# Gate and up of 18 feature tiles as seven block products, and the second gate moved to finished blocks

## The chip, the cores and the metric

The kernel runs on one core of a Trainium2 chip. Its time is the device time of one execution in microseconds; three runs of the kernel before gave 1183.9 to 1186.93 us, with a median of 1185.81 us. The engines are TensorE (PE, with its weight loads as PEld), VectorE (DVE), ScalarE (ACT), GpSimd (POOL) and SyncE (SP), which issues most transfers.

## The reference, cut to what matters

One decoder layer in float32 on 1024 tokens of width 1024: a normalization modulated by a conditioning vector, a mixer (windowed attention beside a state-space scan), a gated residual, then the part that the change touches:

```
def swiglu(h, w_gate_up, w_down):
    gu = h @ w_gate_up
    g, u = gu[..., :D_FF], gu[..., D_FF:]
    return (jax.nn.silu(g) * u) @ w_down          # D_FF = 2816 = 22 tiles of 128

h = rmsnorm(x, norm2[l]) * (1.0 + scale2) + shift2
x = x + gate2 * swiglu(h, w_gate_up[l], w_down[l])
return rmsnorm(x, final_norm)
```

`gate2` is one row of 1024 numbers, `cond @ ada_w[:, section 5]` plus a bias; it scales the columns of the down projection's result.

## The kernel before, in words

Every large matrix product is done in three partial products: an operand is split into a high part (a cast on ScalarE, line 89) and a low part (a subtraction on VectorE, line 80), and `mm3` (lines 92 to 95) multiplies high by high, high by low and low by high, each a matmul of a 128x128 weight with a 128x512 right-hand side.

The 1024 tokens are two halves of 512. The normalized and transposed input of the feed-forward part is `h2[half][kt]`: two halves, eight contraction tiles of 128, each as high and low part in the buffer FR, made by `h_tile` in `second_norm` (lines 701 to 714).

Gate and up: for a feature tile f and a half, `gate_up` (lines 721 to 733) loads and splits the gate weights and the up weights of the tile (512 KB each), runs 8 x 3 matmuls for each, and then forms SiLU of gate (ScalarE) times up (VectorE, line 83). The first four tiles (`early = 4`) do half 0 early, between other work, and half 1 in the main loop of lines 817 to 832; the other 18 tiles do both halves there. Two tiles form a pair. When a pair is done, `act_sums` makes four sums or differences of its four blocks on GpSimd, and seven blocks are stored to memory (`act_d`).

Down: the same scheme of seven products in place of eight is there already (Winograd's form of Strassen's method, on 2x2 blocks: pairs of feature tiles by token halves and by column halves of the result). `dn_weight` loads a pair's down weights, multiplies them by `gate2` on GpSimd (line 795), forms t1 to t4 on GpSimd (lines 798 to 801) and stores seven blocks (`wdn_d`). The stage after the loop runs seven products (`dna` to `dng`) of 11 steps, each step 12 matmuls on two operands read back from memory and split; at each product's end its four banks are added into the rows `yo` (lines 893 to 929), the residual `x1` is added on GpSimd, and squares for the last normalization are taken on ScalarE.

`second_gate` computes the row `gate2` in pieces behind tiles 1 to 8: loads of 512 KB of `ada_rest`, a multiply-add on VectorE (line 408), and at the end two matmuls (`gate`, lines 410 to 414).

Order: transfers issued by `dma` keep their written order on SP, and one that has to wait holds up all behind it. On the compute engines a planner at build time may take an instruction ahead of others written before it, by its estimate of when operands are ready; on the chip each engine then works in that order. Buffers are views at fixed offsets (in KB) of the large tiles FR, FP, FA, FB and GF; a tile opened on memory of a closed pool waits for all users of the old one. `Ring` hands out slots in turn.

Of the kernel before, what the change touches and what calls it, by code (L numbers as in the profile page):

```python
# [33 lines left out]
FR_N, FP_N, FA_N, FB_N, GF_N = 109 * 256 + 128, FP_MISC + 3072, 70 * 256 + 8, 6480, 92 * 256  # L34
# [3 lines left out]
def hymba_layer(ctx: ExitStack, tc: tile.TileContext, x, ada01, ada_rest, w_qk, w_vz, w_xbc,  # L38
# [483 lines left out]
    def ssd_prep(half):  # L522
# [31 lines left out]
        zh = view(FR, 108, [P])  # L554
# [4 lines left out]
        vt = view(FR, 108.5 + 0.5 * half, [P])  # L559
# [108 lines left out]
    hf_ring = ring_at(FA, 66.03125, 2, 2)  # L668
# [32 lines left out]
    def second_norm(half, xr, ss):  # L701
        xn = []
        for t in range(4):
            s1 = ring([1], "ss1", 4)
            add(s1, ss[t][:, 0:1], ss[t][:, 1:2])
            r = rstd_of(s1, D, f"r2_{half}{t}", 1)
            n = xn_buf[half][t]
            for e in range(2):
                es = slice(512 * e, 512 * e + 512)
                nc.vector.tensor_scalar(out=n[:, es], in0=xr[t][:, es], scalar1=r, scalar2=None, op0=ALU.mult)  # L710
            dma(x1_d[4 * half + t], xr[t])
            xn.append(n)
        for kt in range(KT):
            h_tile(h2[half][kt], xn, kt, g2, sh2, hf_ring([512]), f"h2{half}_{kt}", sm_bank, nc.vector.tensor_copy)
# [3 lines left out]
    wdn_d = {(j, i): DR.tile([P, 512], F32, tag=f"wdnd{j}_{i}", name=f"wdnd{j}_{i}") for j in ("b11", "b21", "b22", "t1", "t2", "t3", "t4") for i in range(NP)}  # L718
    early = 4

    def gate_up(f, half, out):
        pss = []
        for s in range(2):
            if (f, s) not in resident:
                resident[(f, s)] = load_w(w_gu[f + NF * s], [KT, P])
            h, l = resident[(f, s)]
            ps = mm_bank(f"psgu{f}{s}{half}")
            for kt in range(KT):
                t = h2[half][kt]
# [34 lines left out]
    pre = {(f, s): load_w(w_gu[f + NF * s], [KT, P]) for f, s in ((0, 0), (0, 1), (1, 0))}  # L764
    second_norm(1, xr, ss)
    flush()
    p_f1.close()
    p_g = ctx.enter_context(tc.tile_pool(name="p_g", bufs=1))
    GF = p_g.tile([P, GF_N], F32, name="GF")
    pair_ring, s_ring = ring_at(GF, 4, 8, 2), ring_at(GF, 20, 8, 2)  # L770
    bw_ring, bt_ring = ring_at(GF, 36, 8, 2), ring_at(GF, 52, 8, 2)
    gate2, grow2 = view(GF, 68, [D]), view(GF, 72, [D])
    resident = dict(pre)

    def second_gate(kks):
# [12 lines left out]


    def dn_weight(i):  # L790
        w, t = bw_ring([4, 512]), bt_ring([4, 512])
        for r in range(2):
            rows = w[:, 2 * r:2 * r + 2].rearrange("p a b -> p (a b)")
            dma(rows, w_dn[(2 * i + r) * P:(2 * i + r + 1) * P, :])
            nc.gpsimd.tensor_tensor(out=rows, in0=rows, in1=gate2, op=ALU.mult)  # L795
        b11, b12, b21, b22 = (w[:, k] for k in range(4))
        t1, t2, t3, t4 = (t[:, k] for k in range(4))
        gsub(t1, b12, b11)
        gsub(t2, b22, t1)
        gsub(t3, b22, b12)  # L800
        gsub(t4, b21, t2)
        for j, v in (("b11", b11), ("b21", b21), ("b22", b22), ("t1", t1), ("t2", t2), ("t3", t3), ("t4", t4)):
            store(wdn_d, j, i, v)

    def act_sums(i, a):
        s = s_ring([4, 512])
        a11, a12, a21, a22 = (a[:, k] for k in range(4))
        s1, s2, s3, s4 = (s[:, k] for k in range(4))
        gadd(s1, a21, a22)
        gsub(s2, s1, a11)  # L810
        gsub(s3, a11, a21)
        gsub(s4, a12, s2)
        for j, v in (("a11", a11), ("a12", a12), ("a22", a22), ("s1", s1), ("s2", s2), ("s3", s3), ("s4", s4)):
            if 2 * i >= early or j not in ("a11", "a12"):
                store(act_d, j, i, v)

    for i in range(NP):
        a = pair_ring([4, 512])
        for r in range(2):
            f = 2 * i + r  # L820
            if f < early:
                dma(a[:, r], act_d["a12" if r else "a11", i])
            else:
                gate_up(f, 0, a[:, r])
            gate_up(f, 1, a[:, 2 + r])
            flush()
            if 1 <= f <= 8:
                second_gate([f - 1])
            if 0 <= f - 10 < NP:
                dn_weight(f - 10)  # L830
# [4 lines left out]
    yo = [view(GF, 4 * t, [D]) for t in range(8)]  # L835
    x1 = [view(GF, 36 + 4 * t, [D]) for t in range(8)]
    op_ring = Ring([(FR, 48 + 4 * i) for i in range(4)] + [(FR, 4 * i) for i in range(12)] + [(FR, 64 + 4 * i) for i in range(10)])
    rawd_ring = ring_at(GF, 76, 2, 8)
    sq_ring = ring_at(GF, 68, 2, 2)
    fnb = view(GF, 72, [D])  # L840
# [7 lines left out]

    def product(ja, jb, banks, late, at):
# [4 lines left out]
        for i in range(NP):  # L854
            ab = operand(act_d[ja, i]), operand(wdn_d[jb, i])
# [10 lines left out]

    lo, hi = slice(0, 512), slice(512, 1024)
    sqs = [ring([2], "ssf", 8) for t in range(8)]

    def square(t, e):  # L870
        nc.scalar.activation(sq_ring([512]), yo[t][:, (lo, hi)[e]], AF.Square, accum_out=sqs[t][:, e:e + 1])

    def finish_row(t):
# [19 lines left out]
    p1 = product_into(mm_bank, "dna", "a11", "b11")  # L893
    flush()
    for t in range(4):
        nc.scalar.copy(yo[t][:, hi], p1[t])
    for t in range(8):
        dma(x1[t], x1_d[t])
    p2 = product_into(sm_bank, "dnb", "a12", "b21")
    for t in range(4):  # L900
        add(yo[t][:, lo], yo[t][:, hi], p2[t])
        gadd(yo[t][:, lo], yo[t][:, lo], x1[t][:, lo])
        square(t, 0)
    p6 = product_into(mm_bank, "dnc", "s2", "t2")
    dma(fnb, fnorm.partition_broadcast(P))
    for t in range(4):
        add(yo[t][:, hi], yo[t][:, hi], p6[t])
    p7 = product_into(sm_bank, "dnd", "s3", "t3")
    for t in range(4):
        add(yo[t + 4][:, hi], yo[t][:, hi], p7[t])  # L910
    p4 = product_into(mm_bank, "dne", "a22", "t4")
    for t in range(4):
        add(yo[t + 4][:, lo], yo[t + 4][:, hi], p4[t])
        gadd(yo[t + 4][:, lo], yo[t + 4][:, lo], x1[t + 4][:, lo])
        square(t + 4, 0)
    p5 = product_into(sm_bank, "dnf", "s1", "t1")
    for t in range(4):
        add(yo[t + 4][:, hi], yo[t + 4][:, hi], p5[t])
        add(yo[t][:, hi], yo[t][:, hi], p5[t])
        gadd(yo[t][:, hi], yo[t][:, hi], x1[t][:, hi])  # L920
        gadd(yo[t + 4][:, hi], yo[t + 4][:, hi], x1[t + 4][:, hi])
        square(t + 4, 1)
    p3 = product_into(mm_bank, "dng", "s4", "b22", 4, {5: lambda: [finish_row(t) for t in range(4, 8)]})
    put()
    for t in range(4):
        add(yo[t][:, hi], yo[t][:, hi], p3[t])
# [67 lines left out]
```

## Time and profile before

| | |
|---|---|
| median of three runs | 1185.81 us |
| profiled execution, its own time | 1182.94 us |
| its span | 1181.1 us |
| TensorE busy | 1145.7 us (97%), 5592 matmuls |
| VectorE, ScalarE, GpSimd busy | 604.6, 456.6, 251.5 us |
| main gate-and-up loop | about 520 to 962 us |
| down stage | 962 us to the end |

"L93" is line 93 of the kernel. A row such as `psgu<-FR` names the tile written and the tile read. Durations of matmuls overlap, so counts in a stretch of time say more than their mean. A bracket at the end of a timeline row is the idle time before the first of its instructions and what ended it.

### The profile page before, as it was taken

The numbers are of one execution on the slowest core, as the hardware profiler recorded it, in microseconds if no ns is written. First come the engines' busy times: TensorE is split into PE (matmuls) and PEld (weight loads), VectorE is DVE, ScalarE is ACT, GpSimd is POOL, SyncE is SP. The second block draws the span as 40 slices with busy tenths as digits, with TensorE's granted clock in tenths as the row PEclk, the third lists the DMA queues.
The fourth block names the chain that finished last, engine by engine and source line by source line (L and its number), as shares of the span: only waits on it lengthen the run. The fifth ranks groups of instructions, "written<-read, shape, count | busy, mean of one in ns | idle before, by whom it ended". The sixth has DMA issues, their size and how long they took to land.

```text
span 1181.1 us, 15303 instructions
## 1 busy us (share of the span) xinstructions
PE 1145.7 (97%) x5592; PEld 946.1 (80%) x5592; DVE 604.6 (51%) x1166; ACT 456.6 (39%) x883; POOL 251.5 (21%) x184
## 2 busy tenths in 40 slices
PE   7999999999999899999999999999999999999996
PEld 6789977777878687887888888888888888888885
DVE  6976278789854865473213212222212165755555
ACT  4672266665656465342111211111111145644530
POOL 0000000002100121002110117558557520200231
PEclk9999999999999999999999999999999999999998
DMA  7546544320510541336423416566566689866523
GB/s 275 183 152 223 190 152 161 111 77 18 187 37 1 193 146 55 117 125 218 157 77 119 143 57 238 211 227 237 208 237 222 221 278 351 292 208 195 168 83 143
DMA packets 80591, 197.56 MB, mean 167 GB/s; under 512 B 9170, under 2 KB 10242, under 8 KB 80388
## 3 DMA queue, kind: packets, MB, share of 16 engines
q1 hardware_dynamic: 76612, 189.40, 46.1%
q10 hardware_dynamic: 3904, 7.18, 1.8%
q8 instruction: 44, 0.72, 0.2%
q14 instruction: 31, 0.25, 0.1%
HBM read 145.68 MB, written 52.44 MB: 168 GB/s over the span
## 4 chain that ended last, share of the span: by engine, by line
PE 71%; DVE 4%; ACT 3%; POOL 1%; issue 1%; DMA 0%; SPq 0%; DVEq 0%; POOLq 0%; ACTq 0%
PE psgu L93 13%; PE psgu L95 13%; PE psgu L94 13%; PE wo L95 2%; PE wo L93 2%; PE wo L94 2%; PE psy L485 1%; DVE FB L83 1%; PE ydg L612 1%; PE dnf L95 1%; PE dnf L93 1%; PE dne L95 1%; PE dne L93 1%; PE dnd L95 1%; PE dnd L93 1%
## 5 line engine op out<-in xcount | busy, mean ns | idle before, releaser
L93 PE MATMUL psgu<-FR 128*128 128x512 f32 x704 | 275.6, 392 | 2.4 <-ACT FR L89 2.4
L95 PE MATMUL psgu<-FR 128*128 128x512 f32 x704 | 275.5, 391 | 0.0
L94 PE MATMUL psgu<-FR 128*128 128x512 f32 x704 | 275.1, 391 | 0.0
L89 ACT CAST FR<-FP 128x1024 fp32r<-128x1024 f32 (+2 forms) x75 | 76.3, 1021 | 266.0 <-DMA FP<-in_w_gu 118.2
L80 DVE TENSOR_TENSOR FR<-FP,FR 128x1024 fp32r<-128x1024 f32 (+3 forms) x83 | 100.9, 1219 | 140.3 <-ACT FR L89 139.5
L93 PEld LDWEIGHTS psgu<-FR 128*128 128x128 f32 x704 | 132.4, 188 | 30.6 <-ACT FR L89 3.3
L94 PEld LDWEIGHTS psgu<-FR 128*128 128x128 f32 x704 | 132.6, 188 | 28.3 <-DVE FR L80 0.9
L95 PEld LDWEIGHTS psgu<-FR 128*128 128x128 f32 x704 | 132.4, 188 | 28.5 <-DVE FR L80 0.8
L80 DVE TENSOR_TENSOR FR<-GF,FR 128x512 fp32r<-128x512 f32 x154 | 107.7, 737 | 80.6 <-ACT FR L89 79.8
L784 POOL TENSOR_TENSOR GF<-GF 128x512 f32<-128x512 f32 x77 | 107.8, 1415 | 90.6 <-DVE GF L83 87.5
L89 ACT CAST FR<-GF 128x512 fp32r<-128x512 f32 x154 | 89.8, 621 | 90.3 <-DMA GF<-actda 26.9
L145 POOL TENSOR_TENSOR FP<-FP 128x1 f32<-128x1 f32 (+1 forms) x40 | 28.4, 715 | 408.9 <-DVE FP L144 354.8
L83 DVE TENSOR_TENSOR GF<-GF,psgu 128x512 f32<-128x512 f32 x40 | 27.4, 685 | 150.9 <-PE psgu L95 150.9
L787 POOL TENSOR_TENSOR GF<-GF 128x512 f32<-128x512 f32 x27 | 37.0, 1389 | 289.2 <-DVE GF L83 129.8
L795 POOL TENSOR_TENSOR GF<-GF 128x1024 f32<-128x1024 f32 x22 | 60.8, 2764 | 53.3 <-DMA GF<-in_w_dn 53.3
L732 ACT ACTIVATE GF<-psgu 128x512 f32<-128x512 f32 x40 | 23.7, 593 | 118.5 <-PE psgu L95 70.5
L93 PE MATMUL psx<-FR 128*128 128x512 f32 x128 | 52.2, 408 | 0.0
L94 PE MATMUL psx<-FR 128*128 128x512 f32 x128 | 51.9, 405 | 0.0
L95 PE MATMUL psx<-FR 128*128 128x512 f32 x128 | 51.7, 404 | 0.0
L95 PE MATMUL wo<-FR 128*128 128x512 f32 x128 | 51.1, 400 | 0.0
L93 PE MATMUL wo<-FR 128*128 128x512 f32 x128 | 51.1, 402 | 0.0
L94 PE MATMUL wo<-FR 128*128 128x512 f32 x128 | 51.0, 400 | 0.0
(290 smaller groups left out, 2076.9 us busy)
## 6 DMA issues: line engine op xcount, KB each, us to landing
FP<-in_w_gu SPq DMA_DIRECT2D x52, 512.0 KB, 5.6
FP<-in_ada_rest SPq DMA_DIRECT2D x32, 512.0 KB, 4.2
actds<-GF SPq DMA_DIRECT2D x44, 256.0 KB, 2.2
GF<-in_w_dn SPq DMA_DIRECT2D x22, 512.0 KB, 4.6
wdndt<-GF SPq DMA_DIRECT2D x44, 256.0 KB, 2.3
GF<-actds SPq DMA_DIRECT2D x44, 256.0 KB, 3.9
GF<-wdndt SPq DMA_DIRECT2D x44, 256.0 KB, 3.5
GF<-actda SPq DMA_DIRECT2D x37, 256.0 KB, 3.9
```

Of the source, the lines that this page charges most:

```text
L80: nc.vector.tensor_tensor(out=out, in0=a, in1=b, op=ALU.subtract)
L83: nc.vector.tensor_tensor(out=out, in0=a, in1=b, op=ALU.mult)
L89: nc.scalar.copy(h, raw)
L93: nc.tensor.matmul(ps, lhsT=lh, rhs=rh, start=first, stop=False)
L94: nc.tensor.matmul(ps, lhsT=lh, rhs=rl, start=False, stop=False)
L95: nc.tensor.matmul(ps, lhsT=ll, rhs=rh, start=False, stop=last)
L145: nc.gpsimd.tensor_tensor(out=r, in0=r, in1=mhalf[:, 0:count], op=ALU.pow)
L485: nc.tensor.matmul(py[:, h * 64:(h + 1) * 64], lhsT=pT[:, h, b], rhs=v_sb[tk][:, 64 * g:64 * g + 64], start=(b == 0), stop=(b == nk - 1))
L732: nc.scalar.activation(out, pss[0], AF.Silu)
L784: nc.gpsimd.tensor_tensor(out=out, in0=a, in1=b, op=ALU.subtract)
L787: nc.gpsimd.tensor_tensor(out=out, in0=a, in1=b, op=ALU.add)
L795: nc.gpsimd.tensor_tensor(out=rows, in0=rows, in1=gate2, op=ALU.mult)
```

## The change

Gate and up of tiles 4 to 21 take the seven-product form too, with blocks along the contraction: the gate weights and the up weights of a tile are the two block rows, the lower and upper four contraction tiles the two block columns, and the token halves are the columns of the right-hand side. One product is 4 contraction tiles x 3 matmuls into one PSUM bank; seven of them make gate and up for both halves.

- The right-hand sides: four of the seven need sums of h2 blocks (t1 to t4). `second_norm` now also stores every block to memory (16 stores from ScalarE's queue); during the first four tiles the blocks are loaded back, and `h2_sums` makes 16 sums and splits them.
- The weights: `w_operand` makes one split operand for each product, five products ahead, four of the seven after a sum on VectorE. Raw weights are fetched ahead (`fetch`) into a ring of three.
- The outputs: `gate_up7` adds the products on VectorE (one copy and two SiLUs on ScalarE).
- `dn_weight` no longer multiplies by the gate; only t1 to t4 are stored, the plain blocks are read from the weights themselves. `act_sums` works with one set of buffers.
- Down stage: `second_gate` runs at steps of products 1 and 2, after the buffers of the gate-and-up part are given up (`open_gd`, at step 4 of product 1, behind the last stores). The products come in another order; a block that is complete except for the last product is multiplied by `gate2` and gets its residual (`residual`); the last product's right-hand blocks are multiplied by `gate2` ahead of time on GpSimd (`gated_load`), so its result is added after the gating. The rings of raw and split operands have 6 and 15 slots (before 8 and 26).

```diff
     def second_norm(half, xr, ss):
...
         for kt in range(KT):
-            h_tile(h2[half][kt], xn, kt, g2, sh2, hf_ring([512]), f"h2{half}_{kt}", sm_bank, nc.vector.tensor_copy)
+            hf = hf_ring([512])
+            h_tile(h2[half][kt], xn, kt, g2, sh2, hf, f"h2{half}_{kt}", sm_bank, nc.vector.tensor_copy)
+            nc.scalar.dma_start(h2_d[half][kt], hf)
...
+    wanted = order[3:] + [(f, s) for f in range(early, NF) for s in range(2)]
+    def fetch():
+        if wanted:
+            f, s = wanted.pop(0)
+            fetched[f, s] = raw_ring([KT, P])
+            dma(fetched[f, s], w_gu[f + NF * s])
...
     def dn_weight(i):
...
-            nc.gpsimd.tensor_tensor(out=rows, in0=rows, in1=gate2, op=ALU.mult)
...
-        for j, v in (("b11", b11), ("b21", b21), ("b22", b22), ("t1", t1), ("t2", t2), ("t3", t3), ("t4", t4)):
+        for j, v in (("t1", t1), ("t2", t2), ("t3", b12), ("t4", t4)):
             store(wdn_d, j, i, v)
...
+    def h2_sums(k):
+        b11, b12, b21, b22, t1, t2 = h2_set[k % 2]
+        for o, v, a, b in ((op_t1, t1, b12, b11), (op_t2, t2, b22, t1), (op_t3, b12, b22, b12), (op_t4, b21, b21, t2)):
+            sub(v, a, b)
+            split(o[k][:, 0], o[k][:, 1], v)
...
+    def w_operand(n):
+        f, j = divmod(n, 7)
+        f += early
+        if f >= NF:
+            return
+        g, u = fetched[f, 0], fetched[f, 1]
+        a11, a12, a21, a22 = g[:, 0:4], g[:, 4:8], u[:, 0:4], u[:, 4:8]
+        if j == 2:
+            add(s1_w, a21, a22)
+            sub(s2_w, s1_w, a11)
+        elif j == 4:
+            sub(s3_w, a11, a21)
+        elif j == 5:
+            sub(s2_w, a12, s2_w)
+        v = (a11, a12, s2_w, s1_w, s3_w, s2_w, a22)[j]
+        w = w_ring([2, 4, P])
+        split(w[:, 0], w[:, 1], v)
+        w_ops[n] = w
+        if j > 4:
+            fetch()
+    AHEAD = 5
+    rhs = (h2[0][0:4], h2[0][4:8], op_t2, op_t1, op_t3, h2[1][4:8], op_t4)
+    def gate_up7(f, out0, out1):
+        u = u_ring([512])
+        for j in range(7):
+            n = 7 * (f - early) + j
+            w_operand(n + AHEAD)
+            w, ps = w_ops.pop(n), (mm_bank, sm_bank)[n % 2](f"psg7_{j}_{f}")
+            for k in range(4):
+                mm3(ps, w[:, 0, k], w[:, 1, k], rhs[j][k][:, 0], rhs[j][k][:, 1], k == 0, k == 3)
+            if j == 0:
+                nc.scalar.copy(u, ps)
+            elif j == 1:
+                add(c11, u, ps)
+                nc.scalar.activation(c11, c11, AF.Silu)
+            elif j == 2:
+                add(u, u, ps)
+            elif j == 3:
+                add(u4, u, ps)
+            elif j == 4:
+                add(out1, u4, ps)
+                add(u, u, ps)
+            elif j == 5:
+                add(u4, u4, ps)
+                nc.scalar.activation(u4, u4, AF.Silu)
+                mul(out1, out1, u4)
+            else:
+                add(out0, u, ps)
+                mul(out0, out0, c11)
...
             if f < early:
                 dma(a[:, r], act_d["a12" if r else "a11", i])
+                h2_sums(f)
+                if f + 2 < 4:
+                    h2_load(f + 2)
+                gate_up(f, 1, a[:, 2 + r], lambda s: early_then(f, s))
             else:
-                gate_up(f, 0, a[:, r])
-            gate_up(f, 1, a[:, 2 + r])
+                gate_up7(f, a[:, r], a[:, 2 + r])
             flush()
-            if 1 <= f <= 8:
-                second_gate([f - 1])
-            if 0 <= f - 10 < NP:
-                dn_weight(f - 10)
+            if 0 <= f - 9 < NP:
+                dn_weight(f - 9)
...
+    def open_gd():
+        flush()
+        p_g.close()
+        return ctx.enter_context(tc.tile_pool(name="p_gd", bufs=1)).tile([P, GD_N], F32, name="GD")
...
+    def residual(t, e, eng=None):
+        es = (lo, hi)[e]
+        (eng or gmul)(rows[t][e], rows[t][e], gate2[:, es])
+        gadd(rows[t][e], rows[t][e], x1[t][:, es])
...
+    p1 = product_into(mm_bank, "dna", "a11", "b11", 0, {4 + 2 * kk: lambda kk=kk: second_gate(kk) for kk in range(4)})
...
+    p2 = product_into(sm_bank, "dnb", "a12", "b21", 0, {2 * kk - 7: lambda kk=kk: second_gate(kk) for kk in range(4, 8)})
...
+    p5 = product_into(sm_bank, "dnd", "s1", "t1", 0, {i: lambda i=i: gated_step(i) for i in range(NP)})
...
+    p7 = product_into(sm_bank, "dne", "s3", "t3", 0, late_steps)
     for t in range(4):
+        add(yc[t], ya[t], p7[t])
+        add(ya[t], yd[t], p7[t])
+        residual(t + 4, 1)
+        residual(t, 1)
+        square(t + 4, 1)
...
+    p3 = product_into(mm_bank, "dng", "s4", "b22g", 4, {5: lambda: [finish_row(t) for t in range(4, 8)]})
```

## Rows read from the trace of the kernel before

**Rows 1.** The page: busy time, and 40 slices (tenths; GB/s).
```profile
PE 1145.7 (97%) x5592; PEld 946.1 (80%) x5592; DVE 604.6 (51%) x1166; ACT 456.6 (39%) x883; POOL 251.5 (21%) x184
...
PEclk9999999999999999999999999999999999999998
...
GB/s 275 183 152 223 190 152 161 111 77 18 187 37 1 193 146 55 117 125 218 157 77 119 143 57 238 211 227 237 208 237 222 221 278 351 292 208 195 168 83 143
```

**Rows 2.** The page: the chain that ended last, by engine and by line.
```profile
PE 71%; DVE 4%; ACT 3%; POOL 1%; issue 1%; DMA 0%; SPq 0%; DVEq 0%; POOLq 0%; ACTq 0%
PE psgu L93 13%; PE psgu L95 13%; PE psgu L94 13%; PE wo L95 2%; PE wo L93 2%; PE wo L94 2%; PE psy L485 1%; DVE FB L83 1%; PE ydg L612 1%; PE dnf L95 1%; PE dnf L93 1%; PE dne L95 1%; PE dne L93 1%; PE dnd L95 1%; PE dnd L93 1%
```

**Rows 3.** Windows: length, each engine's busy us (instructions), clock, DMA share, GB/s.
```profile
800.00:900.00 100.00, 100.00 (x443) 82.77 (x442) 21.89 (x20) 15.16 (x19) 65.22 (x38) 1.00 0.60 219
...
1000.00:1100.00 100.00, 100.00 (x443) 82.81 (x442) 62.95 (x97) 51.60 (x92) 6.49 (x4) 1.00 0.72 236
```

**Rows 4.** Tile psgu: ns min/median/max, first and last start.
```profile
L95 PE MATMUL psgu<-FR x704: 388/389/792, 404.3 to 962.3; 128*128 128x512 f32 x176
```

**Rows 5.** Timeline of PE from 555: start us, us, instruction, [idle before].
```profile
556.30 0.79 PE L93 MATMUL psgu<-FR 128*128 128x512 f32 x1 [2.08 <-ACT FR L89]
556.88 0.63 PE L94 MATMUL psgu<-FR 128*128 128x512 f32 x1
...
559.00 0.63 PE L95 MATMUL psgu<-FR 128*128 128x512 f32 x1
559.43 0.55 PE L93 MATMUL psgu<-FR 128*128 128x512 f32 x1
559.81 0.39 PE L94 MATMUL psgu<-FR 128*128 128x512 f32 x1
```

**Rows 6.** Lines L80, L83, L784 (700 to 940), L80 (990 to 1140), page's cast.
```profile
L80 DVE TENSOR_TENSOR FR<-FP,FR x22: 1224/1226/3454, 714.7 to 936.4; 128x1024 fp32r<-128x1024 f32 x22
...
L83 DVE TENSOR_TENSOR GF<-GF,psgu x22: 675/687/689, 701.7 to 930.2; 128x512 f32<-128x512 f32 x22
...
L784 POOL TENSOR_TENSOR GF<-GF x61: 1279/1291/2287, 703.8 to 940.0; 128x512 f32<-128x512 f32 x61
...
L80 DVE TENSOR_TENSOR FR<-GF,FR x125: 679/691/1779, 990.0 to 1137.9; 128x512 fp32r<-128x512 f32 x125
...
L89 ACT CAST FR<-GF 128x512 fp32r<-128x512 f32 x154 | 89.8, 621 | 90.3 <-DMA GF<-actda 26.9
```

**Rows 7.** Timeline of DVE from 527.
```profile
527.27 0.69 DVE L80 TENSOR_TENSOR FR<-FA,FR 128x512 fp32r<-128x512 f32 x1
532.78 0.69 DVE L83 TENSOR_TENSOR GF<-GF,psgu 128x512 f32<-128x512 f32 x1 [4.82 <-PE psgu L95]
...
543.38 0.69 DVE L83 TENSOR_TENSOR GF<-GF,psgu 128x512 f32<-128x512 f32 x1 [1.08 <-PE psgu L95]
```

**Rows 8.** Timeline of SP's queue from 528.
```profile
528.10 0.80 SPq L71 DMA_DIRECT2D GF<-actda  x2
```

**Rows 9.** The page: transfers, count, KB each, median us to landing.
```profile
FP<-in_w_gu SPq DMA_DIRECT2D x52, 512.0 KB, 5.6
...
actds<-GF SPq DMA_DIRECT2D x44, 256.0 KB, 2.2
...
GF<-actds SPq DMA_DIRECT2D x44, 256.0 KB, 3.9
```

**Rows 10.** Line L615, a transfer issued from ScalarE.
```profile
L615 ACTq DMA_DIRECT2D FA<-gzd x8: 326/326/327, 148.1 to 435.4; - x8
```

**Rows 11.** Line L408, the second gate's multiply-add.
```profile
L408 DVE SCALAR_TENSOR_TENSOR GF<-FP,GF x7: 1281/1285/1287, 552.9 to 665.5; 128x1024 f32<-128x1024 f32 x7
```

**Rows 12.** Timeline of DVE from 955.
```profile
958.65 4.76 DVE L80 TENSOR_TENSOR FR<-GF,FR 128x512 fp32r<-128x512 f32 x7 [4.91 <-ACT FR L89]
963.33 0.68 DVE L83 TENSOR_TENSOR GF<-GF,psgu 128x512 f32<-128x512 f32 x1
```

**Rows 13.** Tile dng, the last product.
```profile
L95 PE MATMUL dng<-FR x44: 388/389/389, 1142.5 to 1171.8; 128*128 128x512 f32 x44
```

More of the change, by code (lines that the diff above doesn't have):

```diff
@@ L667, in hymba_layer @@
     wot_ring = Ring([(FA, 52), (FB, 22)])
-    hf_ring = ring_at(FA, 66.03125, 2, 2)
+    h2_d = [[DR.tile([P, 512], F32, tag=f"h2d{half}_{kt}", name=f"h2d{half}_{kt}") for kt in range(KT)] for half in range(2)]
     sq_half = view(FB, 12, [512])
@@ L731, in gate_up @@
             pss.append(ps)
+            if then:
+                then(s)
         nc.scalar.activation(out, pss[0], AF.Silu)
@@ L764, in hymba_layer @@
     pre = {(f, s): load_w(w_gu[f + NF * s], [KT, P]) for f, s in ((0, 0), (0, 1), (1, 0))}
+    order = [(f, s) for f in range(early) for s in range(2)]
+    wanted = order[3:] + [(f, s) for f in range(early, NF) for s in range(2)]
+    fetched = {}
+    def fetch():
[3 more added lines that the diff above has]
+            dma(fetched[f, s], w_gu[f + NF * s])
+    for _ in range(3):
+        fetch()
     second_norm(1, xr, ss)
@@ new lines, in h2_sums, with early_load @@
+    def h2_sums(k):
[3 more added lines that the diff above has]
+            split(o[k][:, 0], o[k][:, 1], v)
+    resident = dict(pre)
+    def early_load(n):
+        if n < len(order):
+            hl = ws_ring([2, D])
+            h, l = (hl[:, j].rearrange("p (a b) -> p a b", a=KT) for j in range(2))
+            split(h, l, fetched.pop(order[n]))
+            resident[order[n]] = h, l
+            fetch()
@@ L817, in hymba_layer, with early_then @@
+    def early_then(f, s):
+        nonlocal w_ring
+        early_load(2 * f + 3 + s)
+        if f == early - 1:
+            if s == 0:
+                k0 = ws_ring.i
+                w_ring = Ring([(FR, ws_ring.slots[(k0 + d) % 3][1] + e) for d in range(3) for e in (0, 4)] + [(FR, 16 + 4 * k) for k in range(4)])
+            for n in ((0, 1, 2, 3), (4,))[s]:
+                w_operand(n)
+    w_ring = None
+    h2_load(0)
+    h2_load(1)
     for i in range(NP):
@@ L891, in product_into, with gates @@
         return p
-    p1 = product_into(mm_bank, "dna", "a11", "b11")
-    flush()
-    for t in range(4):
-        nc.scalar.copy(yo[t][:, hi], p1[t])
-    for t in range(8):
+    def gates():
+        gate(5, [gate2[:, 0:512], gate2[:, 512:1024]], grow2)
+    p1 = product_into(mm_bank, "dna", "a11", "b11", 0, {4 + 2 * kk: lambda kk=kk: second_gate(kk) for kk in range(4)})
+    ya, yb, yc, yd = ([view(GD, 8 * t + 2 * k, [512]) for t in range(4)] for k in range(4))
+    rows = [(yb[t], yd[t]) for t in range(4)] + [(yc[t], ya[t]) for t in range(4)]
```

153 lines of the change are left out of this document (94 added, 59 removed).

## The prediction, made before the changed kernel ran

> **What bounds the kernel now.** I read the page's busy shares first, then the slices, the chain of waits, then a table by windows, because a busy share does not say at what rate an engine works. TensorE is busy 97% of the span and granted full clock in nearly every slice [rows 1]; the chain runs through it for 71%, and three lines of gate-and-up matmuls (`psgu`) are 13% each [rows 2]. The reader must not take a matmul's duration, 389 ns [rows 4], as its price: matmuls overlap. The window 800 to 900 holds 443 of them in 100 us with TensorE never idle [rows 3], so one costs 100/443 = 0.2257 us. The down stage keeps the same pace (443 in 1000 to 1100, [rows 3]). In both stages VectorE is far from full: 22 and 63 of 100 us. So what counts is the number of matmuls, as long as VectorE, ScalarE and the transfers keep their operands ahead of them.
>
> **What goes.** A feature tile before is 2 halves x 2 (gate, up) x 8 contraction tiles x 3 partial products = 96 matmuls; after, 7 products x 4 x 3 = 84. For tiles 4 to 21 that is 18 x 12 = 216 matmuls fewer, 216 x 0.2257 = 48.8 us, all on the chain. A new tile takes 84 x 0.2257 = 19.0 us of TensorE (before 21.7), one product 2.71 us.
>
> A second gain: at 556.30 TensorE had stood 2.08 us for a weight cast, and its next seven steps took 559.81 - 556.30 = 3.5 us instead of 7 x 0.226 = 1.6 [rows 5]: a gap of 2.1 us cost 4.0. There the in-order transfer queue issues loads of the second gate's rows ahead of the next weights. After, these rows are loaded in the down stage and weights are fetched ahead, so I take 4.0 off; if something new is late there, nothing.
>
> **What comes on VectorE in a new tile.** Operands: seven low parts and four sums, SBUF to SBUF, 11 x 0.69 the 128x512 split of [rows 6]; outputs: seven additions from PSUM and two multiplications, 9 x 0.69 the L83 row of [rows 6]. 20 x 0.69 = 13.8 us of 19.0. Before it was two splits of 1.23 and two multiplications, 3.8 us. ScalarE gets seven casts, a copy and two SiLUs, ten operations of some 0.62 us the cast in [rows 6], far below 19. Operands are made five products (13.6 us) ahead and eight PSUM banks take turns, so single waits are covered; the cover is gone only if VectorE's average passes 19.0 us.
>
> It can be pushed there by GpSimd. A 128x1024 split takes 1.226 us at the median but up to 3.454 us in the window where GpSimd is busiest, while operations that read PSUM stay within 675 to 689 ns [rows 6]. So 13 of the 20 new operations can be held up by a GpSimd subtraction (1.29 us, [rows 6]), seven cannot. In tiles 9 to 19 GpSimd has per pair of tiles 2 x 4 subtractions of down weights and 4 of activations, 12 x 1.29 = 15.5 of 38 us, 41%. A random meeting costs half a subtraction: 13 x 0.41 x 0.65 = 3.4 us, VectorE 17.2 of 19.0. At worst all six subtractions of a tile stand in its way: 13.8 + 7.7 = 21.5 us, 2.5 us too much in 11 tiles, 27 us. At best nothing. Between 0 and 27 I take 1, since the likely 17.2 is below 19.0.
>
> The Trainium skill (SBUF — State Buffer, Who interferes with whom) says why: VectorE and GpSimd share one port pair, an exclusive lock that a VectorE instruction with two SBUF inputs contends for with a GpSimd instruction that reads SBUF, and the loser blocks fully. The rows above agree, with 3.454 us for a split that takes 1.226 alone. By this rule the change replaces long, sparse operations by many that need the lock, and it is the strongest thing against it; what it would cost is the rival B below.
>
> **The first four tiles.** They keep 192 matmuls (43 us), but VectorE now makes the right-hand operands beside them: 4 x (4 sums + 4 low parts) = 32 x 0.69 = 22 us, with five weight splits of 1.23, four multiplications and the first seven operand steps: 22 + 6.2 + 2.8 + 4.8 = 35.8 us. The normalized blocks go out through memory and come back: the last is done at 527.27 + 0.69 = 528.0, and at 528.1 the queue could first write the new buffers [rows 7, 8]; a store (2.2) and a load (3.9, [rows 9]) put the first sums at 534. The tiles end near 565 (532.8 + 3 x 10.8 by the multiplications, [rows 7], without the gap). Two splits fit before 534, so 33 us stand against 31: VectorE ends 2 us late. But the first new product needs the plain blocks alone, and the last of the sums are due 16 us later. What could be late are weights behind the sums in the queue. Bounds 0 and 4 us (a gap like that of [rows 5]); I take 1. The 16 stores issue from ScalarE at 0.33 us [rows 10], where each waits beside 1.06 us of VectorE per block: nothing.
>
> **The down stage** keeps its 924 matmuls. The second gate's eight steps of 1.29 us [rows 11] lie beside products 1 and 2, in which 22 splits take 15 of 29.8 us. Its 4 MB replace the x1 loads there, which had the queue at 351 GB/s in a slice [rows 1]; a product wants 5.8 MB in 29.8 us, 193 GB/s, plus 0.5 MB every two steps (5.4 us), 97: 290 GB/s, below that.
>
> One new wait counts. At the fifth step of product 1 the queue stores the last activation sums, then loads into buffers that overlie the old ones, and every operand from the sixth step on is behind it. After the last matmul (962.3 + 0.4, [rows 4]) come an addition, a multiplication, a subtraction (0.7 + 0.7 + 1.3), the store 2.2, two issues, the load 3.9, a cast and a low part: about 13 us. TensorE has five steps, 13.5 us. Bounds 0 and 4 us; I take 1. For the order I go by the trace: seven splits of the next stage stand ahead of the last multiplication on VectorE [rows 12], so independent work is moved forward past such waits.
>
> Applying the gate to blocks puts 12 multiplications on GpSimd and 4 on VectorE (0.7 us each) at product ends, and 11 on GpSimd for the last operand. After product 5 of the written order (`dne`) that is 16 GpSimd operations, 20.6 us; if each of some 16 splits waits for one (0.69 + 1.29), VectorE is 7 splits short in 32 us, and the ring of 15 operands covers 7. Cost 0, without that cover 5. After the last matmul (1171.8, [rows 13]) the same additions, squares, scalings and stores follow: 9.3 us of the span as before.
>
> **The sum.** Against the profiled execution (1182.94 us: span 1181.1 and 1.84 around it): 1182.94 - 48.8 - 4.0 + 1 + 1 + 1 = 1133.1. It was 2.9 us below the median of the runs, 1185.81, so I predict 1136.
>
> **Rivals.** B, the lock decides: VectorE needs 21.5 us in tiles 9 to 19, TensorE waits for operands there, +27 at the bound: 1162, half of it 1149. For it the 3.454 us row and 41% GpSimd; against it the median of 1.226 us with GpSimd busier than it will be (about 65% in the window 800 to 900, [rows 3]). Chance 0.13.
> C, two or three gaps of the kind in [rows 5] (first tiles, the queue's wait in product 1, the first product), 4 us each with the slower clock behind it: 1136 - 3 + 3 x 4 = 1145, or 1141 with two. For it the margins of -2 and +0.5 us; against it the five-product lead. Chance 0.13.
> D, slower: VectorE passes 21.7 us per tile, TensorE's old time, so that it stops in every product and does not come back to full clock. At the lower level, 1.2 of 2.4 GHz, a step took about 0.43 us [rows 5], a tile 84 x 0.43 = 36 us; in half of each of 11 tiles that is 11 x 8.6 = 94 us: 1230. It decides only if all GpSimd operations and more hit, and a slower TensorE gives VectorE time to catch up. Chance 0.04.
> E, better: nothing of the three unit terms comes, and the other transfers shift favourably: 1129 to 1132 or less. Chance 0.04. That the number of matmuls does not fall is excluded by the code.
>
> **How the numbers follow.** The forecast, 1131 to 1141, has 0.65; B and C 0.13 each, D and E 0.04, and 0.01 lies between B and D. The range reaches from E to the half of B: 1129 to 1152. A measurement tells 0.3%, 3.6 us, from no change: faster 0.95 (forecast, B, C, E), same 0.01, slower 0.04 (D).
>
> **What would show it.** 216 matmuls fewer at an unchanged pace of 443 per 100 us between the last of the first four tiles and product 1; VectorE busy 73 to 90% there; no gap at the place of [rows 5]; longest splits of 2 us beside GpSimd without TensorE waiting; the five steps of product 1 just covering the store. It is wrong if TensorE waits for VectorE's low parts in tiles 9 to 19, or the granted clock falls inside the stage.

## The result and the profile after

The changed kernel took 1147.72 us (median; runs 1144.76, 1144.90, 1150.54, 1150.87), the kernel before, timed beside it, 1185.49 us. The ratio is 0.968, 95% interval 0.9645 to 0.9719. 37.8 us are gone; the forecast was 49.8. The time lies in the range (1129 to 1152) but above the forecast's own (1131 to 1141). Its profiled execution took 1144.76 us, with a span of 1143.0.

The page of the changed kernel, engines and the granted clock by slice; before: [rows 1].

```profile
PE 1105.0 (97%) x5376; PEld 912.4 (80%) x5376; DVE 842.6 (74%) x1490; ACT 517.2 (45%) x1007; POOL 244.6 (21%) x185
...
PEclk9999999999999969999999999999999999999998
```

There are 216 matmuls fewer, as counted, and VectorE is 74% busy where it was 51%. One slice, the 15th (400 to 429 us), shows a clock of 6 where every slice before had 9; it is the first sign of what went wrong.

Windows of the changed kernel: length, busy us of PE, PEld, DVE, ACT and POOL (instructions), granted clock, DMA share, GB/s; before: [rows 3].

```profile
640.00:880.00 240.00, 240.00 (x1060) 198.75 (x1059) 203.51 (x253) 75.41 (x125) 107.74 (x68) 1.00 0.57 197
800.00:900.00 100.00, 100.00 (x443) 82.79 (x442) 82.85 (x102) 30.31 (x51) 44.00 (x28) 1.00 0.56 192
1000.00:1100.00 100.00, 98.83 (x435) 81.29 (x434) 76.30 (x97) 50.52 (x90) 40.72 (x27) 1.00 0.73 240
```

In the stage of 18 tiles TensorE never stops, at the old pace of 443 in 100 us. In the down stage it lost 1.2 us in one window.

What the matmuls waited for, 395 us to the end, changed kernel (us in total, times, longest), gate-and-up and down products:

```profile
PE psgu L94 <- DVE FR L179: 1.3, 3, 0.5
PE psgu L94 <- ACT FR L90: 1.1, 1, 1.1
PE dna L94 <- ACT FR L90: 1.1, 1, 1.1
PE dnf L94 <- ACT FR L90: 0.9, 1, 0.9
PE psgu L96 <- DVE FR L81: 0.5, 1, 0.5
PE dnf L95 <- DVE FR L81: 0.2, 1, 0.2
```

No wait of the new products (`psg`) is among them. Cut at the start of the first gate-and-up matmul, then at the start of the last matmul of each stage, the two spans divide like this:

| stretch | before, us | after, us | difference |
|---|---|---|---|
| start to first gate-and-up matmul | 402.6 | 412.2 | +9.6 |
| to the end of the first four tiles | 166.3 | 164.3 | -2.0 |
| 18 tiles | 393.4 | 342.7 | -50.7 |
| down stage | 209.4 | 214.3 | +4.9 |
| tail | 9.3 | 9.4 | +0.1 |

The middle came as forecast; 14.5 us were lost at its two ends. The loss at the first shows on ScalarE. Timeline (start, us, instruction, [idle before]) of the kernel before, ScalarE, then TensorE; the rows `ps_h` make the normalized blocks, and the first of them is the first block:

```profile
398.72 1.45 ACT L190 ACTIVATE FA<-ps_h,FP 128x512 f32<-128x512 f32 x2 [4.68 <-PE ps_h L184]
...
401.48 1.03 ACT L89 CAST FR<-FP 128x1024 fp32r<-128x1024 f32 x1
402.42 1.45 ACT L190 ACTIVATE FA<-ps_h,FP 128x512 f32<-128x512 f32 x2
403.75 1.05 ACT L89 CAST FR<-FP 128x1024 fp32r<-128x1024 f32 x1
...
402.57 0.50 PE L93 MATMUL psgu<-FR 128*128 128x512 f32 x1 [0.28 <-ACT FR L89]
```

The same of the changed kernel:

```profile
400.45 1.45 ACT L191 ACTIVATE FA<-ps_h,FP 128x512 f32<-128x512 f32 x2 [4.68 <-PE ps_h L185]
401.26 1.00 ACTq L718 DMA_DIRECT2D h2d<-FA  x2
402.31 1.45 ACT L191 ACTIVATE FA<-ps_h,FP 128x512 f32<-128x512 f32 x2 [0.40 <-PE ps_h L185]
...
411.08 2.96 ACT L90 CAST FR<-FP 128x1024 fp32r<-128x1024 f32 x3
...
412.21 0.79 PE L94 MATMUL psgu<-FR 128*128 128x512 f32 x1 [1.14 <-ACT FR L90]
```

Before, the first weight casts stood between the blocks of `second_norm`; now all eight blocks with their stores, and six instructions of the scan, come first, and the casts at 411.08 follow without a wait of their own. TensorE runs short of work meanwhile. Windows 410 to 420, of the kernel before:

```profile
410.00:415.00 5.00, 5.00 (x30) 4.06 (x29) 4.94 (x7) 1.20 (x3) 1.61 (x2) 1.00 0.91 306
415.00:420.00 5.00, 5.00 (x25) 4.18 (x25) 3.73 (x6) 3.35 (x5) 0.63 (x1) 1.00 0.58 220
```

and of the changed one, where TensorE stood still for a third of the time and the clock is at its lower level, 0.50 of full (1.2 of 2.4 GHz), before it comes back (it was at 0.50 in 400 to 405 us already, where the kernel before had 1.00):

```profile
410.00:415.00 5.00, 3.27 (x10) 1.82 (x8) 3.96 (x6) 4.05 (x6) 1.30 (x2) 0.50 0.00 0
415.00:420.00 5.00, 5.00 (x19) 4.54 (x19) 1.85 (x3) 0.00 (x0) 1.61 (x1) 0.50 0.31 105
420.00:425.00 5.00, 5.00 (x18) 3.93 (x18) 3.85 (x6) 1.02 (x4) 0.70 (x1) 0.73 0.40 118
```

### The profile page after: what moved, and what is told of

It reads as the page before. It is cut to its first block, busy times and chain, and to the rows that moved or that the text cites. A ratio compares the mean times of both kernels' runs of the same rounds, so it can differ in the third digit from the quotient of the medians.

```text
span 1143.0 us, 15497 instructions
## 1 busy us (share of the span) xinstructions
PE 1105.0 (97%) x5376; PEld 912.4 (80%) x5376; DVE 842.6 (74%) x1490; ACT 517.2 (45%) x1007; POOL 244.6 (21%) x185
## 5 line engine op out<-in xcount | busy, mean ns | idle before, releaser
L81 DVE TENSOR_TENSOR FR<-FP,FR 128x512 fp32r<-128x512 f32 (+4 forms) x244 | 195.0, 822 | 68.8 <-ACT FR L90 68.3
L90 ACT CAST FR<-FP 128x512 fp32r<-128x512 f32 (+3 forms) x236 | 157.7, 682 | 185.6 <-PE psg L95 79.8
L94 PE MATMUL psg<-FR 128*128 128x512 f32 x306 | 119.0, 389 | 0.0
L95 PE MATMUL psg<-FR 128*128 128x512 f32 x306 | 119.0, 389 | 0.0
L96 PE MATMUL psg<-FR 128*128 128x512 f32 x306 | 119.0, 389 | 0.0
L87 DVE TENSOR_TENSOR GF<-GF,psg 128x512 f32<-128x512 f32 x126 | 84.2, 680 | 30.4 <-PE psg L96 27.9
L90 ACT CAST FR<-GF 128x512 fp32r<-128x512 f32 x77 | 47.4, 619 | 79.8 <-PE psg L95 54.5
L94 PE MATMUL psg<-GR,FR 128*128 128x512 f32 x198 | 77.0, 389 | 0.0
L95 PE MATMUL psg<-GR,FR 128*128 128x512 f32 x198 | 77.0, 389 | 0.0
L96 PE MATMUL psg<-GR,FR 128*128 128x512 f32 x198 | 77.0, 389 | 0.0
L95 PEld LDWEIGHTS psg<-FR 128*128 128x128 f32 x306 | 57.4, 188 | 12.0
L94 PEld LDWEIGHTS psg<-FR 128*128 128x128 f32 x306 | 57.4, 188 | 11.9
L96 PEld LDWEIGHTS psg<-FR 128*128 128x128 f32 x306 | 57.4, 188 | 11.9
L803 POOL TENSOR_TENSOR GD<-GD 128x512 f32<-128x512 f32 x23 | 35.7, 1562 | 119.7 <-ACT GD L415 57.7
L94 PE MATMUL psgu<-FR 128*128 128x512 f32 x128 | 51.6, 407 | 2.5 <-DVE FR L179 1.3
L94 PE MATMUL psx<-FR 128*128 128x512 f32 x128 | 52.2, 408 | 0.0
L96 PE MATMUL psgu<-FR 128*128 128x512 f32 x128 | 51.4, 403 | 0.5 <-DVE FR L81 0.5
L95 PE MATMUL psx<-FR 128*128 128x512 f32 x128 | 51.8, 405 | 0.0
```

What stands on the lines that cost most here:

```text
L81: nc.vector.tensor_tensor(out=out, in0=a, in1=b, op=ALU.subtract)
L87: nc.vector.tensor_tensor(out=out, in0=a, in1=b, op=ALU.add)
L90: nc.scalar.copy(h, raw)
L94: nc.tensor.matmul(ps, lhsT=lh, rhs=rh, start=first, stop=False)
L95: nc.tensor.matmul(ps, lhsT=lh, rhs=rl, start=False, stop=False)
L96: nc.tensor.matmul(ps, lhsT=ll, rhs=rh, start=False, stop=last)
```

## The experiments

All ratios are to the kernel before, timed beside each kernel on the same chip. Not all of them ran on one chip, so two kernels are compared by their ratios, and they differ where the intervals don't overlap. Only one execution of each kernel has a profile.

**The changed kernel once more**, as the base of what follows.

> The changed kernel unchanged, for comparison on one chip. Its four runs lie at 1144.8, 1144.9 and 1150.5, 1150.9. Theory (the slower clock after the late weight casts of the first gate-and-up tile lasts longer or shorter from run to run): two groups again, some 6 us apart, median 1145 to 1151. Rival (scatter from elsewhere): one group.

1146.01 us (1144.98 to 1147.66), ratio 0.9673 [0.9657, 0.9688]. The two groups of times of the first measurement did not return. The shape is the same: gate and up from 411.6, the new tiles from 577.0, `dna` without a gap, `dnf` 33.3 us.

**The ring of four alone.** `second_norm` of the change also gave the blocks four buffers for two, which the prediction had not seen.

```diff
-    hf_ring = ring_at(FA, 66.03125, 2, 2)
...
+        hf_ring = Ring([(FA, 66.03125), (FA, 68.03125)] + ([(FA, 10), (FA, 12)], [(FA, 32), (FA, 34)])[half])
```

> The kernel before with nothing but the ring of four blocks in second_norm (two before), no stores to memory. Theory A: the ring lets ScalarE make the normalized blocks one after another, and the planner puts the first weight casts behind all eight; TensorE starts the first gate-and-up matmul near 410 us in place of 402.6, at the lower clock level: 5 to 9 us slower than before, 1191 to 1195. Theory B (the stores on ScalarE's queue and their traffic are what costs): within 1.5 us of before, 1184 to 1187.

1188.26 us, ratio 1.0029 [1.0016, 1.0043]: 2.7 us slower than the kernel before. The first gate-and-up matmul started at 407.92:

```profile
398.66 4.80 ACT L190 ACTIVATE FA<-ps_h,FP 128x512 f32<-128x512 f32 x7 [4.68 <-PE ps_h L184]
...
406.81 1.06 ACT L89 CAST FR<-FP 128x1024 fp32r<-128x1024 f32 x1
...
407.92 0.50 PE L93 MATMUL psgu<-FR 128*128 128x512 f32 x1 [1.81 <-ACT FR L89]
```

With two buffers casts stood between the blocks; with four, seven blocks run together and the casts come behind. That the planner had filled ScalarE's stops between blocks with casts is inferred from this order. So the ring alone moves the casts, 5.3 us later, and half of that reaches the end. The order is that of theory A, at about half its price; the time lies between the two that were expected.

**The ring and the stores**, both put into the kernel before.

```diff
+            nc.scalar.dma_start(h2_d[half][kt], hf)
```

> The kernel before with the ring of four blocks and the 16 stores of blocks to memory from ScalarE's queue (nothing reads them). The ring alone cost 2.7 us (e1). Theory (ring and stores together make the loss ahead of the first tiles): the first gate-and-up matmul starts at 411 to 412 us as in the changed kernel (402.6 before, 407.9 with the ring alone), and the time is 1192 to 1196. Rival (the stores add nothing; the rest of the loss comes from the other edits): 1187 to 1190.

1190.81 us, ratio 1.0042 [1.0028, 1.0055], 5.0 us slower than the kernel before; the first matmul started at 412.74, as late as in the changed kernel (412.21). ScalarE, then TensorE:

```profile
401.00 1.45 ACT L190 ACTIVATE FA<-ps_h,FP 128x512 f32<-128x512 f32 x2 [4.68 <-PE ps_h L184]
...
412.74 0.80 PE L93 MATMUL psgu<-FR 128*128 128x512 f32 x1 [0.68 <-ACT FR L89]
```

This confirms the place; the price lies between the two that were expected, and the interval overlaps that of the ring alone, so a price of the stores by themselves is not shown in the time.

**The first weights ahead of the blocks**, in the changed kernel.

```diff
     xr, ss = out_proj(0)
+    resident.update({(0, s): load_w(w_gu[NF * s], [KT, P]) for s in range(2)})
     second_norm(0, xr, ss)
```

> The changed kernel with the gate and up weights of tile 0 loaded and split before second_norm of half 0; ring and stores stay. Theory A: the casts stand ahead of the blocks, TensorE starts on the first blocks and keeps its clock: 6 to 10 us faster than the changed kernel, 1136 to 1141, in one group of times. Theory B: the stores stay, so the loss stays: within 2 us of the changed kernel.

1140.30 us, ratio 0.9615 [0.9599, 0.9631]: 5.7 us faster than the changed kernel, with intervals apart and just under the 6 to 10 expected. The first matmul is back at 403.24, behind the first two blocks, and the first four tiles end at 571.5 (576.5). ScalarE, then TensorE:

```profile
401.64 1.45 ACT L191 ACTIVATE FA<-ps_h,FP 128x512 f32<-128x512 f32 x2 [4.82 <-PE ps_h L185]
...
403.24 0.78 PE L94 MATMUL psgu<-FR 128*128 128x512 f32 x1
```

This kernel, called the early-weights kernel below, is the base of the later ones.

**No sums on GpSimd.** In the changed kernel `act_sums` and the sums of `dn_weight` are left out, and other blocks are stored in their places.

> The changed kernel without the GpSimd sums of act_sums and dn_weight in the main loop; the raw blocks are stored in their place (same transfers), so these sums are left out of the result. Theory of the prediction: the long splits beside GpSimd are covered by the five-product lead; the splits fall to 0.69 us each, VectorE's busy share between 640 and 880 us falls from 86% to about 75%, and the time stays within 2 us of the changed kernel (a microsecond may go at the step 5 wait of product 1, where one subtraction is in the chain). Rival (the lock paces the stage): 5 us or more faster.

1144.78 us, ratio 0.9663 [0.9646, 0.9680]; against 1146.01 for the changed kernel that is 1.2 us, and the intervals overlap. The window without GpSimd's sums:

```profile
640.00:880.00 240.00, 240.00 (x1061) 198.79 (x1060) 160.94 (x253) 76.42 (x125) 0.00 (x0) 1.00 0.58 196
```

The splits of line 81 in it, in ns (min/median/max):

```profile
L81 DVE TENSOR_TENSOR FR<-GF,FR x49: 684/686/694, 641.6 to 870.1; 128x512 fp32r<-128x512 f32 x49
...
L81 DVE TENSOR_TENSOR GF<-FP,GF x12: 682/683/687, 653.7 to 863.2; 128x512 f32<-128x512 f32 x12
```

The same lines of the changed kernel, and GpSimd's sums in it:

```profile
L81 DVE TENSOR_TENSOR FR<-GF,FR x50: 676/684/1782, 640.2 to 875.5; 128x512 fp32r<-128x512 f32 x50
...
L81 DVE TENSOR_TENSOR GF<-FP,GF x12: 677/1778/1786, 656.1 to 866.8; 128x512 f32<-128x512 f32 x12
...
L797 POOL TENSOR_TENSOR GF<-GF x62: 1286/1736/1834, 653.9 to 871.4; 128x512 f32<-128x512 f32 x62
```

The long splits, up to 1.78 us, are gone and VectorE is busy 160.9 us in place of 203.5 (67%, where about 75% was expected), but TensorE does the same number of matmuls. Rival B falls: VectorE and GpSimd do hold each other up (GpSimd's sums have a median of 1.74 us, before 1.29 [rows 6]), and here it costs nothing that can be measured.

**The second gate later**, in the early-weights kernel, so that the loads which wait for the stores don't stand ahead of the sixth step's.

```diff
-    p1 = product_into(mm_bank, "dna", "a11", "b11", 0, {4 + 2 * kk: lambda kk=kk: second_gate(kk) for kk in range(4)})
+    p1 = product_into(mm_bank, "dna", "a11", "b11", 0, {6 + 2 * kk: lambda kk=kk: second_gate(kk) for kk in range(3)})
...
+    p2 = product_into(sm_bank, "dnb", "a12", "b21", 0, {2 * kk - 6: lambda kk=kk: second_gate(kk) for kk in range(3, 8)})
```

> e2 (early weights) with the second gate's rows loaded two steps later: from step 6 of product 1, the last at step 8 of product 2. Theory (the queue's wait for the last activation store keeps the sixth step's operands 1.1 us too long): product 1 runs without a gap, 29.9 us in place of 31.2, and the time falls by about 1.3 us, to 1139. Rival (the transfers are the limit there, not the wait): the gap only moves, same time as e2 (1140.3) within 0.5 us.

1138.30 us, ratio 0.9605 [0.9591, 0.9619], 2.0 below the early-weights kernel (1.2 by the ratios) with overlapping intervals. It does not decide: in the early-weights kernel's own profile `dna` has no gap either, so there was nothing to remove.

**The squares later**, in the early-weights kernel. In the changed kernel ScalarE stands in `dnf` (the sixth product) before each of four squares; line 1014, ScalarE:

```profile
1078.38 0.63 ACT L1014 ACTIVATE GD<-GD 128x512 f32<-128x512 f32 x1 [3.99 <-POOL GD L800]
...
1085.17 0.63 ACT L1014 ACTIVATE GD<-GD 128x512 f32<-128x512 f32 x1 [5.04 <-POOL GD L800]
...
1090.61 0.63 ACT L1014 ACTIVATE GD<-GD 128x512 f32<-128x512 f32 x1 [4.71 <-POOL GD L800]
...
1096.50 0.63 ACT L1014 ACTIVATE GD<-GD 128x512 f32<-128x512 f32 x1 [4.13 <-POOL GD L800]
...
1097.13 2.16 ACT L90 CAST FR<-FP 128x512 fp32r<-128x512 f32 x4
```

Behind the last, VectorE and TensorE wait for these casts:

```profile
1091.88 3.44 DVE L81 TENSOR_TENSOR FR<-FP,FR 128x512 fp32r<-128x512 f32 x2 [6.18 <-ACT FR L90]
```

```profile
1097.79 0.51 PE L94 MATMUL dnf<-FR 128*128 128x512 f32 x1 [0.95 <-ACT FR L90]
1098.51 0.50 PE L95 MATMUL dnf<-FR 128*128 128x512 f32 x1 [0.22 <-DVE FR L81]
```

The edit wrote the squares at the ninth step of the product:

```diff
-        square(t + 4, 1)
-    p4 = product_into(sm_bank, "dnf", "a22", "t4")
+    p4 = product_into(sm_bank, "dnf", "a22", "t4", 0, {9: lambda: [square(t + 4, 1) for t in range(4)]})
```

> e2 with the squares of the four rows that wait for GpSimd taken at step 9 of the next product in place of its start. Theory (ScalarE is held by these squares, each waiting for four GpSimd operations, and the casts stand behind them): product dnf runs in 29.9 us in place of 31.7, time down by about 1.7 us, to 1138.6. Rival (VectorE short of splits because of the lock, as the prediction had it): the gap stays, since the GpSimd operations stay; within 0.5 us of e2.

1139.20 us, ratio 0.9614 [0.9600, 0.9629]. The planner put the squares back ahead of the casts (1072.25 to 1090.39), and a gap of 1.31 us in `dnf` remained. The edit did not take effect and tells nothing.

**The residuals in another order**, in the early-weights kernel: first the four rows that are squared, then the other four, so that each square waits for two GpSimd operations in place of four.

```diff
         residual(t + 4, 1)
-        residual(t, 1)
         square(t + 4, 1)
+    for t in range(4):
+        residual(t, 1)
```

> e2 with the residuals at the end of product dne in another order: first the four rows whose squares ScalarE takes, then the other four; same operations. In e5 the planner put the squares ahead of the casts again, so it did not tell. Theory (ScalarE held by squares that wait for GpSimd): the last square comes some 12 us after the product in place of 23, and product dnf takes 30 to 30.5 us in place of 34.9 (e2): time 1136 to 1138. Rival (VectorE short of splits because GpSimd holds the port, the same number of operations): dnf stays at 32 us or more, 1139 to 1141.

1138.56 us, ratio 0.9601 [0.9586, 0.9617], which overlaps that of the early-weights kernel. TensorE's wait for ScalarE in `dnf`, 0.4 to 1.3 us in all nine profiles with the old order, is gone; its wait for VectorE is 1.6 us. `dnf` takes 32.1 us against 34.9 in the early-weights kernel and 29.9 for a plain product, but that alone shows no gain: the nine profiles with the old order lie between 31.1 and 34.9. VectorE, ahead of its late splits:

```profile
1085.90 9.84 DVE L81 TENSOR_TENSOR FR<-FP,FR 128x512 fp32r<-128x512 f32 x9 [6.19 <-ACT FR L90]
```

It stood 6.19 us for a cast that comes behind the last square (1084.63, some 20 us after the product, where 12 were expected); then the first four of the nine splits took 1.74 to 1.77 us each, the others 0.68. So both theories have a part: the squares still hold the casts, and the splits behind them are long beside GpSimd as well. How the rest divides stays open.

**Eight buffers for the second half's blocks**, in the early-weights kernel, since in the changed kernel's `second_norm(1)` ScalarE waits 1.1 to 2.1 us for stores to land before it may write a buffer again.

```diff
-([(FA, 10), (FA, 12)], [(FA, 32), (FA, 34)])[half])
+([(FA, 10), (FA, 12)], [(FA, 32), (FA, 34), (FB, 0), (FB, 2), (FB, 6), (FB, 8)])[half])
```

> e2 with eight buffers for the normalized blocks of half 1 (four before), so that none waits for its store. Theory (ScalarE waits up to 2 us for the landing of stores while the queues are full): the block stage of half 1 takes 9 to 10 us in place of 13.5, and the first tiles end 1.5 to 3 us earlier: 1137.5 to 1139. Rival (the planner, given more buffers, puts weight casts behind the blocks as it did in half 0): same or slower than e2, up to 1144.

1141.34 us, ratio 0.9626 [0.9610, 0.9641]: no gain. The blocks of half 1 did come faster: ScalarE makes them in 10.6 us where it took 12.4 (9 to 10 expected), and TensorE's waits for them (line 179) fell from 1.1 to 0.2 us. But its waits for VectorE's low parts (line 81) rose from 1.7 to 2.3, and the first four tiles end at 571.9 against 571.5. So the stores are not what bounds the end of the first tiles.

**Half of the sums.** In the early-weights kernel t3 and t4 of the right-hand sides are not computed, and t1 and t2 are multiplied in their places.

```diff
-        for o, v, a, b in ((op_t1, t1, b12, b11), (op_t2, t2, b22, t1), (op_t3, b12, b22, b12), (op_t4, b21, b21, t2)):
+        for o, v, a, b in ((op_t1, t1, b12, b11), (op_t2, t2, b22, t1)):
```

> e2 with only t1 and t2 of the h2 sums made; t3 and t4 (16 VectorE operations of 0.69 us, 11 us, and 8 casts) are left out, t1 and t2 stand in for them, so these two products are left out of the result. Theory (VectorE, busy 94% between 550 and 575 us, makes the low parts of the last early weights late): the waits for L81 in the first tiles, 1.7 us with the slower clock behind them, go, and the first tiles end 2 to 4 us earlier: 1136.5 to 1138.5. Rival (the weights' transfers behind the h2 loads are late): the waits stay, within 1 us of 1140.3.

Windows of the early-weights kernel, then of this one (columns as above):

```profile
550.00:575.00 25.00, 23.30 (x102) 18.61 (x101) 23.40 (x33) 13.17 (x22) 6.76 (x4) 1.00 0.73 258
```

```profile
550.00:575.00 25.00, 25.00 (x112) 20.71 (x111) 21.11 (x27) 10.73 (x18) 8.22 (x5) 1.00 0.71 254
```

VectorE was 94% busy there and TensorE lost 1.7 us; with half the sums VectorE is 84% busy, TensorE loses nothing, and the first tiles end at 568.5 (571.5). The profile shows that VectorE is the bound of the first tiles' end. The time does not follow: 1140.86 us (1137.94 to 1143.85), ratio 0.9617 [0.9597, 0.9637], against 1140.30. The profiled execution here was the fastest of its four, that of the early-weights kernel the slowest of its five (1141.71), and the runs of either scatter by 4 to 6 us; whether the 3 us reach the end stays open.

**Three edits together**: early weights, the later second gate, the squares and the eight buffers.

> e2 with all three of e4, e5 and e6. If the three gaps are independent the gains add: 1.3 + 1.7 + 2, 1135 to 1136, faster than both kernels and at the forecast of 1136. If one of them only hides another, 1138 or more.

1138.25 us (1135.57 to 1141.52), ratio 0.9606 [0.9586, 0.9625]: no better than the later second gate alone, as the other two had gained nothing in time.

**The best of them**: early weights, residuals in the new order, the second gate from the sixth step on.

```diff
+    p1 = product_into(mm_bank, "dna", "a11", "b11", 0, {6 + 2 * kk: lambda kk=kk: second_gate(kk) for kk in range(3)})
...
+    p2 = product_into(sm_bank, "dnb", "a12", "b21", 0, {max(0, 2 * kk - 7): lambda kk=kk: second_gate(kk) for kk in range(3, 8)})
```

> e2 with the residual order of e9 and the second gate's rows from step 6 of product 1 (the last at step 7 of product 2). If the gains of early weights, residual order and the freed step add: 1135 to 1137.5, faster than the kernel before and the changed kernel. If run-to-run shifts of the clock ahead of the first tiles cover it: 1138 to 1140.

1137.09 us (1136.58 to 1138.67), ratio 0.9588 [0.9574, 0.9602]. It beats the kernel before by 48.7 us and the changed kernel's second timing by 8.9. Against the early-weights kernel the intervals still overlap, so a gain of the two further edits is not shown. Its waits in the down stage are down to one:

```profile
PE dnf L95 <- DVE FR L81: 0.4, 1, 0.4
```

## Why the prediction was right, and where its sizes were off

**What goes: right.** By the starts of matmuls one costs 0.2267 us, in place of the 0.2257 taken from a count per window, which includes those that overlap its edges. 216 x 0.2267 = 49.0 us; with the second gate's matmuls, which moved out of the stage (1.3 us), that is 50.3 of the 50.7 measured.

**What comes on VectorE: right.** 203.5 of 240 us is 85%, inside the 73 to 90% given. Per tile of 19.0 us that is 16.1 us, without GpSimd 160.9 / 240 x 19.0 = 12.7 (the sum had 17.2 and 13.8); so meetings with GpSimd take 3.4 us a tile, the number of the sum. The Trainium skill (SBUF — State Buffer, Who interferes with whom) has the loser of the lock on the ports that the two share block fully; splits of 1.78 us that shrink to 0.69 without GpSimd agree. Their price to the end, forecast as 1, was nothing that could be measured: TensorE has no wait in the stage, and the 1.2 us of the two medians lie within overlapping intervals. That the five products of lead are what covers it was not tested; no run changed them.

**The first four tiles: near in sum by luck (-2.0, forecast -4 + 1).** The gap of [rows 5] is gone, and VectorE is late at their end, as the 33 against 31 us said. But the stretch in the table is short because it starts late: with the ring and the stores alone, in the kernel before, it is 164.1 us too, and in the early-weights kernel 168.3. It is fairer to count from the first block, since what comes ahead of the blocks shifts by itself. In us, from the profiles:

| kernel | first block at | to the first gate-and-up matmul | to the last matmul of the four tiles |
|---|---|---|---|
| before | 398.7 | 3.8 | 170.2 |
| ring of four alone | 398.7 | 9.3 | 173.8 |
| ring and stores | 401.0 | 11.7 | 175.8 |
| changed | 400.5 | 11.8 | 176.1 |
| early weights | 401.6 | 1.6 | 169.9 |
| early weights, half of the sums | 401.1 | 1.6 | 167.5 |

So the changed kernel loses 5.9 us here, and the ring and the stores alone lose 5.6. With the start repaired 0.3 us are gained, and without half of the sums 2.7 of the 3 forecast: VectorE's lateness, priced at 1, costs 2.4 for that half. The step that failed is the sentence on the 16 stores, "where each waits beside 1.06 us of VectorE per block: nothing". It costed the stores by their 0.33 us of issue and not by what they and the two added buffers do to the order on ScalarE: the casts of the first weights went behind all eight blocks, 7.9 us more between the first block and the first matmul, and TensorE at half clock for much of the time to about 425. In time, the ring and the stores together cost 5.0 us in the kernel before, and early weights gave back 5.7: this is about half of the 12 us between forecast and result.

The other 1.7 of the 9.6 us at the first matmul are there before the blocks. The first block stands at 398.7 in both profiles without the stores and between 399.6 and 405.0 in the twelve with them. In each of the twelve the granted clock is below 1.00 somewhere ahead of 390 us (changed kernel: 0.91 in 40 to 60 us, before 1.00), ahead of anything that the ring or the stores edit, and in the other two it is not. The cause was not tested, and a shift of some 5 us that differs from profile to profile also blurs every comparison of single executions.

**The down stage: +4.9, of which 1.3 is the moved matmuls; forecast +1.** The wait in product 1 came as described, but the 13 us were 14.7. Queue of transfers, then TensorE, changed kernel:

```profile
922.06 3.07 SPq L72 DMA_DIRECT2D actds<-GF  x4
927.27 0.34 SPq L72 DMA_DIRECT2D GD<-in_ada_rest  x1
927.66 0.53 SPq L72 DMA_DIRECT2D FP<-actda  x1
```

```profile
934.29 1.19 PE L94 MATMUL dna<-FR 128*128 128x512 f32 x4 [1.06 <-ACT FR L90]
```

From the end of gate and up (919.6) to the sixth step at 934.29 are 14.7 us, against 13.5 of cover: 1.06 us and a slow start, in some executions only (the second profile of the changed kernel has none). In `dnf` the step that failed is "Cost 0, without that cover 5": the ring of 15 operands was counted against VectorE's splits, but what stood first was ScalarE, whose casts came behind squares that waited for GpSimd; VectorE waited for these casts. It cost 1.8 us in this profile and 3.4 in the second.

**The sum.** On the profiled execution the forecast change was -49.8 (1182.94 to 1133.1), the measured one -38.2 (to 1144.76). The difference of 11.6 is +1.7 ahead of the blocks, +8.9 from there to the end of the first four tiles (+5.9 for -3), -1.9 in the stage (1.3 of moved matmuls and 0.6 of pace and rounding), -1 for the lock, +3.9 in the down stage (4.9 - 1) and +0.1 in the tail; that makes 11.7, with rounding. That the time lies in the range is in part luck: the range was wide because of B and C, B did not come, and half of the miss arose ahead of the first tiles, by an order on ScalarE that no rival named. Rival C's number (1141 to 1145) was nearer than the forecast, but only one of its gaps came in this form, that in product 1. D is excluded by the stage without a wait, and E by the two ends. The four runs of the first timing lie in two pairs, 1144.8 and 1150.7, and the slower pair has the lower mean clock (0.980 and 0.983 against 0.987 and 0.990); in the second, four lie between 1145.0 and 1147.7, and their clocks do not order them. What parts them was not found.

## What to carry to other kernels

Where a planner orders the engines, read for each edited line which instructions filled its stalls: giving a stage more buffers can take away the stalls, and what stood in them, here the casts that the next stage starts with, goes behind it. Price an added operation at the engine's queue, by what is in line behind it, and not by its own duration. VectorE at 85%, slowed by GpSimd, cost nothing here where its consumer was five products behind, but TensorE lost 1.7 us in 25 where VectorE was at 94%. When single executions are compared, count from an instruction that both kernels have just ahead of the edit, here the first block, and not from the start of the span.

## What the runs showed of the hardware that was not expected

- Meetings of VectorE and GpSimd are not random: of the 12 subtractions `GF<-FP,GF` in 640 to 880 us 10 took 1.77 to 1.79 us, while the splits `FR<-GF,FR` beside them kept a median of 684 ns. The operation recurs at one place of the loop and meets GpSimd there most times; the sum had taken half a subtraction per random meeting, and came out right as a mean.
- TensorE's start can come 5.3 us later with only 2.7 us at the end (the ring alone). In the profiles 1.8 us are given back before the first four tiles end (572.45 against 568.88) and 3.5 us remain at the end (1186.47 against 1182.94). So an early gap was not worth its length here; which waits gave it back was not traced.
